# Attention steps reordered: scores, values, transposes, then a layer's products

## The chip, the cores and the metric

One core of a Trainium2 chip runs the whole program. The metric is the device time of one execution in microseconds, taken as the median of several runs. A profiled execution of the same program gives the trace; its time is the span from the first to the last instruction of the program.

## What is computed

A two-layer model on 256 latent and 256 context tokens of width 1024: layer 0 mixes tokens by retention, layer 1 by neighbourhood attention; each has a squared-ReLU MLP of hidden width 4096. The change lies in layer 1's attention, cut here to what matters:

```python
NAT_HEADS, NAT_HEAD_DIM, GRID_W, NAT_WIN_COLS = 32, 32, 64, 16
def row_block(args):                          # one row of 64 queries
    q_r, r = args
    k_band, v_band = ...                      # the rows of the window
    bias = jnp.where(col_in[:, None, :], bias, -jnp.inf)
    s_loc = jnp.einsum('bqhd,bikhd->bhqik', q_r, k_band) + bias
    s_ctx = jnp.einsum('bqhd,blhd->bhql', q_r, k_c)
    prob = jax.nn.softmax(jnp.concatenate([s_loc, s_ctx], -1), axis=-1)
    return (jnp.einsum('bhqik,bikhd->bqhd', p_loc, v_band)
            + jnp.einsum('bhql,blhd->bqhd', prob[..., band:], v_c))
y_lat = o.reshape(b, n, d) @ w_o
```

With 256 latent tokens there are four grid rows, all in every window. The columns of a window are 16 of 64.

## The kernel before

**Products in three parts.** Weights and activations are split into a high part (`hi`, rounded for the fast product) and a low part (`lo`, the rest); a product is three matmuls (`mm3`). `fetch(n)` (L255) issues the loads of the next `n` weight units from SP's queue (512 KB each) and casts each to `hi` on ScalarE (ACT); `lows(n)` (L277) subtracts on VectorE (DVE) to give `lo`. TensorE (PE) runs the products.

**An attention step** handles four heads (a group `g`) and one half of the query columns (`qt`), 16 steps in all. Each step `n` goes through these pieces:

- `scores(n)` (L1543): 12 matmuls in four 32-row tiles of the array, which write four PSUM banks (`pqk`), one a head.
- `soften(n)` (L1556): for each head VectorE adds the bias and takes the row minimum in one instruction (`s<-pqk,bias`), and ScalarE takes the exponential (`s<-s,mn`) with its row sum. `invert(n)` (L1582) takes the reciprocal of the sums and spreads them (`rr`).
- `gather(n)` (L1596): GpSimd copies the few probabilities of the other half's columns to one tile and loads a later step's bias.
- `flip(n)` (L1608): 13 transposes of the probabilities to four banks (`ppt`), three a head and a fourth one in the last; ScalarE copies the first and the third bank to `pt`, VectorE the second and the fourth. `flip_sums` (L1623) transposes the reciprocals to one half of the bank `pav`; `turned(n)` (L1629) copies them to `rt` on ScalarE.
- `attend(n)` (L1634), the values: one full-array matmul on the gathered probabilities and 12 matmuls in four 32-column tiles, accumulated in the other 128 columns of the same half of `pav`; then VectorE multiplies by `rt`, ScalarE casts the result to `oTh`, VectorE subtracts to `oTl`.

**Where TensorE's other work stands.** The loop at L1825 runs over 13 rows of `STEPS`. A turn runs `scores(n + 2)`, the values of step `n`, the transposes of step `n + 1`, and in `run(before)` a product of the layer: a K or Q or V part or a part of the output projection W, mostly 24 matmuls of 512 columns. `k_evac` and the like bring its result out of PSUM: a ScalarE cast (`kT<-pn`), then a VectorE subtraction. `K(6)`, `Q(3)` in turn 9 and `K(7)` in turn 11 make keys and queries for scores of turns 10 and 12. The first three numbers of a row of `STEPS` are the weight units fetched `early`, `late` and `last` in the turn.

**What sets the order.** Here the engines run what the code writes down, in that order; waits are semaphores put in by the framework. PSUM tiles come from one pool of eight banks (L144), of which `pav` is held through the whole stage; a bank is given out again when its readers are done.

```python
    STEPS = [                      # early, late, last, before, after
        (1, 0, 0, [K(2)], []),
        (0, 2, 0, [K(3)], []),
        (0, 2, 0, [K(4)], []),
        (0, 1, 0, [K(5)], []),
        (0, 2, 1, [Q(2)], []),
        (0, 1, 0, [V(0)], []),
        (0, 0, 0, [V(1)], []),
        (0, 0, 0, [V(2)], [REST]),
        (0, 0, 0, [V(3)], []),
        (2, 2, 1, [Q(3), K(6)], []),
        (0, 0, 1, [W00[0]], [W00[1]]),
        (0, 0, 2, [K(7)], []),
        (0, 0, 0, [W01[0]], [W01[1]]),
    ]
```

## Time and profile before

| | |
|---|---|
| median of 3 runs | 1182.22 us (1179.45 to 1182.62) |
| span of the profiled execution | 1177.4 us |
| TensorE busy | 1167.3 us, 99% of the span |
| VectorE, ScalarE, GpSimd busy | 844.6, 480.6, 212.5 us |
| memory read, rate over the span | 189.12 MB, 166 GB/s |

TensorE's clock is granted in full in all 40 slices of the page. In a timeline row stand start in us, length in us, engine, line, operation, tile written and tiles read, shapes and a count; several instructions in a row are merged to one, whose length then goes from the first's start to the last's end. A bracket gives idle time ahead and what ended it. All instructions carry L84, a helper that issues them; tile names tell them apart. A full-precision matmul shows as two passes (x2, x24). Ends of matmuls are modelled, so TensorE's waits are read from starts.

### The profile page before, as it was taken

What the parts mean: (1) busy time and instruction counts of PE and PEld (TensorE: products, weight loads), DVE (VectorE), ACT (ScalarE), POOL (GpSimd) and SP (SyncE); (2) the same over time, 40 slices, a digit from 0 to 9 for tenths busy, and PEclk for the clock granted to TensorE, in tenths of its full rate; (3) what the DMA queues carried; (4) which work ended last, traced back from release to release, by engine and by line L of the source; (5) the groups of instructions that cost most, each with busy time, mean ns of one, the idle gap of its engine ahead of it and who ended that gap; (6) DMA issues with size and microseconds to landing.
All of it is one profiled execution on the core that took longest, in us unless ns stands there. A gap on an engine that the chain in (4) does not pass through costs nothing.

```text
span 1177.4 us, 17745 instructions
## 1 busy us (share of the span) xinstructions
PE 1167.3 (99%) x6821; PEld 985.6 (84%) x6821; DVE 844.6 (72%) x1349; ACT 480.6 (41%) x819; POOL 212.5 (18%) x364
## 2 busy tenths in 40 slices
PE   9999999999999999999999999999999999999997
PEld 7788888888888889888888888889888878999886
DVE  3786678787888787757767675678577589877446
ACT  3643332222323246442212333137466666665341
POOL 0103001000200241780203000223343430000001
PEclk9999999999999999999999999999999999999999
DMA  9943544544355416757566665646344334766660
GB/s 276 276 130 104 161 143 140 152 147 152 118 169 175 141 60 214 189 112 217 171 190 197 212 199 190 201 141 204 83 135 139 111 115 155 222 209 197 233 212 36
DMA packets 140115, 195.10 MB, mean 166 GB/s; under 512 B 9936, under 2 KB 81136, under 8 KB 140032
## 3 DMA queue, kind: packets, MB, share of 16 engines
q1 hardware_dynamic: 131904, 182.03, 49.4%
q0 software_dynamic: 6976, 9.39, 3.9%
q10 hardware_dynamic: 1152, 2.56, 0.7%
q8 instruction: 53, 0.87, 0.3%
q14 instruction: 30, 0.25, 0.1%
HBM read 189.12 MB, written 5.75 MB: 166 GB/s over the span
## 4 chain that ended last, share of the span: by engine, by line
PE 94%; DMA 2%; SPq 1%; ACT 1%; DVE 1%; issue 0%; POOL 0%; ACTq 0%; DVEq 0%
PE p L84 44%; PE pw L84 7%; PE pg L84 7%; PE pq L84 7%; PE pv L84 7%; PE pn L84 5%; PE pnv L84 4%; PE po L84 3%; PE ppt L84 2%; PE pnw L84 1%; PE pS L84 1%; PE pav L84 1%; PE pqk L84 1%; SPq L84 1%; PE pt L84 1%; PE p1t L84 1%
## 5 line engine op out<-in xcount | busy, mean ns | idle before, releaser
L84 ACT CAST hi<-raw 128x1024 fp32r<-128x1024 f32 (+2 forms) x228 | 231.7, 1032 | 308.9 <-PE p L84 113.4
L84 DVE TENSOR_TENSOR lo<-raw,hi 128x1024 fp32r<-128x1024 f32 (+2 forms) x228 | 273.4, 1213 | 105.5 <-ACT hi L84 105.4
L84 PE MATMUL p<-hi,hid 128*128 128x512 f32 (+1 forms) x832 | 241.8, 373 | 0.0
L84 PEld LDWEIGHTS p<-hi,hid 128*128 128x128 f32 x832 | 152.1, 188 | 27.6
L84 PE MATMUL p<-hTh,lo 128*128 128x256 f32 (+1 forms) x512 | 165.8, 326 | 0.0
L84 PE MATMUL p<-hTl,hi 128*128 128x256 f32 (+1 forms) x512 | 165.8, 326 | 0.0
L84 PE MATMUL p<-hTh,hi 128*128 128x256 f32 (+1 forms) x512 | 162.9, 328 | 0.0
L84 PE MATMUL p<-lo,hid 128*128 128x512 f32 (+1 forms) x416 | 155.2, 373 | 0.0
L84 DVE SCALAR_TENSOR_TENSOR acc<-rawa,scol,acc 128x1024 f32<-128x1024 f32 x56 | 74.5, 1342 | 66.0 <-DMA rawa<-in_ada_w_dram 66.0
L84 PEld LDWEIGHTS p<-hTh,lo 128*128 128x128 f32 x512 | 96.4, 188 | 8.8
L84 PEld LDWEIGHTS p<-hTl,hi 128*128 128x128 f32 x512 | 96.4, 188 | 8.7
L84 PEld LDWEIGHTS p<-hTh,hi 128*128 128x128 f32 x512 | 94.2, 188 | 8.7
L84 PEld LDWEIGHTS p<-lo,hid 128*128 128x128 f32 x416 | 78.4, 188 | 13.7
L84 DVE SCALAR_TENSOR_TENSOR strips<-rawa,scol,strips 128x512 f32<-128x512 f32 x112 | 78.6, 762 | 0.0
L84 ACT CAST hid<-r 128x256 fp32r<-128x256 f32 (+1 forms) x64 | 31.9, 500 | 111.2 <-DVE r L84 111.2
L84 POOL TENSOR_TENSOR rstd<-rstd,misc 128x1 f32<-128x1 f32 x28 | 19.1, 684 | 212.4 <-DVE rstd L84 211.4
L84 POOL TENSOR_TENSOR R<-R,acc 128x512 f32<-128x512 f32 x16 | 25.8, 1633 | 168.8 <-DVE acc L84 168.8
L84 ACT ACTIVATE s<-s,mn 128x512 f32<-128x512 f32 x64 | 45.5, 713 | 22.0 <-DVE mn L84 22.0
L84 PE MATMUL pw<-hi,oh 128*128 128x512 f32 x128 | 51.0, 398 | 0.0
L84 PE MATMUL pg<-hi,hTh 128*128 128x512 f32 x128 | 50.6, 395 | 0.0
L84 PE MATMUL pq<-hTh,hi 128*128 128x512 f32 x128 | 49.3, 395 | 0.8 <-ACT hTh L84 0.5
L84 PE MATMUL pw<-hi,ol 128*128 128x512 f32 x128 | 49.9, 390 | 0.0
(238 smaller groups left out, 2278.5 us busy)
## 6 DMA issues: line engine op xcount, KB each, us to landing
raw<-in_mlp_w_dram SPq DMA_DIRECT2D x128, 512.0 KB, 4.2
rawa<-in_ada_w_dram SPq DMA_DIRECT2D x80, 512.0 KB, 3.9
raw<-in_ret_w_in_dram SPq DMA_DIRECT2D x42, 512.0 KB, 3.9
raw<-in_nat_w_in_dram SPq DMA_DIRECT2D x24, 512.0 KB, 4.3
rawq<-in_ada_w_dram SPq DMA_DIRECT2D x16, 512.0 KB, 6.2
raw<-in_ret_w_o_dram SPq DMA_DIRECT2D x16, 512.0 KB, 3.4
bias<-rpb_rows POOLq DMA_DIRECT2D x32, 128.0 KB, 2.9
raw<-in_nat_w_o_dram SPq DMA_DIRECT2D x8, 512.0 KB, 3.8
```

The lines of the kernel that those rows point to most:

```text
L84: r = f(*args, **kwargs)
```

## The change

In a turn the values and the transposes move ahead of the layer's product, directly behind the scores, values first. `soften` stands behind the transposes, `lows(early)` behind `soften`, `invert` behind the layer's product. Within `attend` the full-array matmul goes from the first place to the last.

```diff
@@ attend(n)
-        pe.matmul(po[:, :P], lhsT=rest_values(n), rhs=pt_at(n, NEAR), start=True, stop=False)
         for i, kc in enumerate((qt, 2, 3)):
             for j in range(4):
                 pe.matmul(
...
-                    start=False,
-                    stop=(i == 2),
+                    start=(i == 0),
+                    stop=False,
                     tile_position=(0, 32 * j),
                 )
+        pe.matmul(po[:, :P], lhsT=rest_values(n), rhs=pt_at(n, NEAR), start=False, stop=True)
@@ the loop over STEPS
         gather(n + 1)
         turned(n)
+        scores(n + 2)
+        attend(n)
+        flip(n + 1)
         fetch(early)
+        soften(n + 2)
         lows(early)
-        scores(n + 2)
-        soften(n + 2)
         fetch(late)
         lows(late)
         run(before)
-        flip(n + 1)
         invert(n + 2)
         fetch(last)
-        attend(n)
         run(after)
```

TensorE before, turn 3: from the third group of transposes to the scores of the next turn. The names are those of the pieces above; a wait names the semaphore of an engine (`Activation` is ScalarE).

```order
L84 MATMUL ppt_7631<-cst_81,s_7461 128x128 [waits DVE_49]
L84 MATMUL ppt_7631<-cst_81,s_7461 128x128 x2
L84 MATMUL ppt_7636<-cst_81,s_7464 128x128 [waits DVE_49]
L84 MATMUL ppt_7636<-cst_81,s_7464 128x128 x2
L84 MATMUL ppt_7636<-cst_81,pt_6946 128x128 [waits Pool_49]
L84 MATMUL pav_6943<-cst_81,rr_7529 128x128 [waits Activation_49]
L84 MATMUL pav_6943<-pt_6947,pt_6946 128x128
L84 MATMUL pav_6943<-pt_6947,natv_1079_6942 32x128 x12
L84 MATMUL pqk_7676<-kT_7234,qT_6598 128x512 [waits DVE_49]
```

TensorE in the changed kernel, the same turn, from the last of the scores to the fourth group of transposes:

```order
L84 MATMUL pqk_7561<-kT_7272,qT_6598 128x512
L84 MATMUL pav_6943<-pt_6947,natv_1079_6942 32x128 [waits Activation_49]
L84 MATMUL pav_6943<-pt_6947,natv_1079_6942 32x128 x11
L84 MATMUL pav_6943<-pt_6947,pt_6946 128x128
L84 MATMUL ppt_7590<-cst_81,s_7493 128x128 [waits DVE_49]
L84 MATMUL ppt_7590<-cst_81,s_7493 128x128 x2
L84 MATMUL ppt_7595<-cst_81,s_7496 128x128 [waits DVE_49]
L84 MATMUL ppt_7595<-cst_81,s_7496 128x128 x2
L84 MATMUL ppt_7600<-cst_81,s_7499 128x128 [waits DVE_49]
L84 MATMUL ppt_7600<-cst_81,s_7499 128x128 x2
L84 MATMUL ppt_7605<-cst_81,s_7502 128x128 [waits Activation_49]
```

The values stand ahead of the transposes, their first product waits for ScalarE and so does the fourth group of transposes, which waited for VectorE.

ScalarE in the changed kernel, from the last exponential of turn 4 on (`qT` brings out that turn's layer product, `rt` is `turned(5)`, `oTh` is the cast of `attend(5)`):

```order
L84 ACTIVATE s_7741,sums_7731<-s_7741,mn_7730 128x512 [waits DVE_49]
L84 CAST hi_7746<-raw_7744 128x1024 [waits DMAHW0_49]
L84 CAST hi_7751<-raw_7749 128x1024 [waits DMAHW1_49]
L84 ACTIVATE qT_6598<-pn_7756 128x256 [waits PE_49]
L84 ACTIVATE qT_6598<-pn_7757 128x256 [waits PE_49]
L84 CAST hi_7815<-raw_7813 128x1024 [waits DMAHW2_49,Activation_49]
L84 COPY rt_7827<-pav_6943 128x128 [waits Activation_49]
L84 CAST oTh_6944<-rt_7827 128x4x32 [waits DVE_49]
L84 COPY pt_6946<-ppt_7861 128x384 [waits PE_49,Activation_49]
```

Before, the copies to `pt` stood between `qT` and the last `hi`, and `oTh` ahead of `rt`; now the cast of the values stands between `rt` and the first copy to `pt`.

VectorE in turn 0, before:

```order
L84 COPY rr_7155<-sums_7039 128x128 [waits DVE_49]
L84 TENSOR_TENSOR lo_7201<-raw_7198,hi_7200 128x1024 [waits DMAHW2_49,PE_49,Activation_49]
L84 ISA s_7222,mn_7220<-pqk_7204,bias_6859 128x512 [waits DMASW1_49,DMASW6_49,DMASW0_49,DMASW7_49,PE_49,Pool_49]
L84 ISA mn_7220 128x1
L84 ISA s_7225,mn_7220<-pqk_7205,bias_6859 128x512 [waits PE_49,Pool_49]
```

And in the changed kernel:

```order
L84 COPY rr_7155<-sums_7039 128x128 [waits DVE_49]
L84 TENSOR_TENSOR rt_7196<-pav_6943,rt_7196 128x128 [waits PE_49,Activation_49]
L84 TENSOR_TENSOR oTl_6945<-rt_7196,oTh_6944 128x4x32 [waits Activation_49]
L84 COPY pt_6947<-ppt_7235 128x384 [waits PE_49]
L84 COPY pt_6947<-ppt_7245 128x512 [waits PE_49]
L84 ISA s_7259,mn_7257<-pqk_7198,bias_6859 128x512 [waits DMASW6_49,DMASW1_49,DMASW7_49,DMASW0_49,Pool_49]
L84 ISA mn_7257 128x1
```

The softening, which followed one subtraction, now follows the multiply of the values and the copies of the transposes, and the subtraction `lo` comes behind its fourth head.

## The prediction

> **What bounds the kernel now.** I read the page first, then the stretch of the attention steps (thirteen turns of the loop, 844 to 968 us) step by step, then the timeline of one engine at a time. TensorE runs without a gap and the chain of work that ended last lies on it:

> ```profile
> span 1177.4 us, 17745 instructions
> ...
> PE 94%; DMA 2%; SPq 1%; ACT 1%; DVE 1%; issue 0%; POOL 0%; ACTq 0%; DVEq 0%
> ```

> So whatever makes TensorE wait in these steps is paid in full. Busy time by step (columns: stretch, length, PE, PEld, DVE, ACT, POOL, granted clock, DMA share, GB/s) shows VectorE and ScalarE with two to four us free in each step:

> ```profile
> 853.08:862.20 9.12, 9.12 (x82) 7.38 (x78) 6.48 (x16) 6.64 (x15) 5.16 (x12) 1.00 0.37 84
> 880.59:890.48 9.89, 9.88 (x105) 8.85 (x102) 7.29 (x18) 6.80 (x17) 4.24 (x11) 1.00 0.48 128
> 890.48:900.23 9.75, 9.75 (x80) 7.73 (x77) 7.17 (x18) 6.24 (x15) 3.73 (x10) 1.00 0.65 192
> ```

> That free time is not a queue's slack: both engines work in order, and what counts is when one instruction is reached. One whole turn on TensorE, from the end of a layer's product to the start of the next:

> ```profile
> 868.44 0.39 PE L84 MATMUL pn<-hTh,lo 128*128 128x512 f32 x1
> 868.67 1.47 PE L84 MATMUL ppt<-cst,s 128*128 128x128 f32 x12
> 869.98 0.27 PE L84 MATMUL ppt<-cst,pt 128*128 128x128 f32 x1
> 870.09 0.27 PE L84 MATMUL pav<-cst,rr 128*128 128x128 f32 x1
> 870.20 0.39 PE L84 MATMUL pav<-pt,G 128*128 128x128 f32 x2
> 870.52 0.86 PE L84 MATMUL pav<-pt,natv 128*32 128x128 f32 x24
> 871.31 1.12 PE L84 MATMUL pqk<-kT,qT 32*128 32x512 f32 x12
> 872.36 0.50 PE L84 MATMUL pn<-hTh,hi 128*128 128x512 f32 x1
> ```

> Start to start: 0.23 us for a layer's product, 0.109 for a transpose, 14 transposes 1.53.

> **1. Array switches, about nothing.** A group's last start is its start + its length - the length of one product. Scores (32-row tiles) to the full array: 871.31 + 1.12 - 0.39 = 872.04, next at 872.36: 0.32. Full to 32-column tiles: 870.20 + 0.39 - 0.27 = 870.32, next at 870.52: 0.20. Columns to rows: 870.52 + 0.86 - 0.27 = 871.11, next at 871.31: 0.20. Two switches of the new order stand elsewhere:

> ```profile
> 843.65 0.39 PE L84 MATMUL pnv<-hi,hTl 128*128 128x512 f32 x1
> 843.97 0.97 PE L84 MATMUL pqk<-kT,qT 32*128 32x512 f32 x12
> ```

> ```profile
> 972.35 0.86 PE L84 MATMUL pav<-pt,R 128*32 128x128 f32 x24
> 973.14 1.09 PE L84 MATMUL ppt<-cst,s 128*128 128x128 f32 x8
> ```

> Full to rows 0.32; scores unhindered 0.97 - 0.39 = 0.58; columns to full 973.14 - (972.35 + 0.86 - 0.27) = 0.20. There are three switches a turn before and after. Rows to columns is not shown: between 0.20 and 0.38 (the wait less or more than the rows-to-full one by what the shown kinds differ); I take 0.32, since the same products have to leave. The quiet old turn of 9.12 less 1.53 (transposes), 0.32 (full product and switch), 0.59 + 0.20 (values and switch) and 0.58 + 0.32 (scores and switch) leaves 5.58 for the layer; 0.10 of it is the longer first product (872.36, 0.50 against 0.39) that follows a switch and 0.23 the step to the transposes, so from its first to its last start it takes 5.25 behind transposes. The new turn on TensorE alone, from the last layer product: 0.32 + 0.58 + 0.32 + 0.59 + 0.20 + 0.27 (the full product's two passes, with 0.05 for being first after a switch: 973.14 spaces its eight by 0.117) + 1.53 + 5.25 = 9.06. Thirteen times -0.06: **-0.8**. The tail gets one switch more (values now end full, then scores): +0.2.

> **2. What the old order waits for goes.** Scores followed values directly and waited for the copies of the transposes:

> ```profile
> 880.59 1.47 PE L84 MATMUL pqk<-kT,qT 32*128 32x512 f32 x12
> ```

> ```profile
> 890.48 1.61 PE L84 MATMUL pqk<-kT,qT 32*128 32x512 f32 x12
> 892.02 0.50 PE L84 MATMUL pnv<-hi,hTh 128*128 128x512 f32 x1
> ```

> Against 0.97: 0.15 + 0.50 + 0.64 = **-1.3**. Now a layer's product (5.2 us) stands before the scores.

> **3. The fourth group of transposes waits for a bank, each turn.** Eight banks, one held by `pav`; the four of the new scores stay full until VectorE softens them, which now stands behind the copies of the transposes. Three are left for four groups, and the order shows the fourth group waiting for ScalarE: the copy of the first. Before that copy ScalarE must cast the values:

> ```profile
> 879.10 0.58 ACT L84 CAST kT<-pn 128x512 fp32r<-128x512 f32 x1
> 879.57 0.85 ACT L84 COPY pt<-ppt 128x384 f32<-128x384 f32 x2
> 882.76 0.30 ACT L84 CAST oTh<-rt 128x128 fp32r<-128x128 f32 x1 [2.34 <-DVE rt L84]
> 882.97 0.26 ACT L84 COPY rt<-pav 128x128 f32<-128x128 f32 x1
> ```

> ```profile
> 872.15 1.14 DVE L84 COPY pt<-ppt 128x384 f32<-128x384 f32 x2
> 873.21 0.17 DVE L84 RECIPROCAL sums<-sums 128x4 f32<-128x4 f32 x1
> 873.48 0.23 DVE L84 COPY rr<-sums 128x128 f32<-128x128 f32 x1
> 873.63 0.28 DVE L84 TENSOR_TENSOR rt<-pav,rt 128x128 f32<-128x128 f32 x1
> ```

> From the start of the full product's second pass: 0.27 till it ends, 0.03 handover, 0.28 multiply, 0.03, 0.21 (cast, next start), 0.48 copy, 0.03 = 1.33. TensorE is there after 0.11 + 9 x 0.109 = 1.09. Wait 0.24, thirteen times: **+3.2**.

> **4. Values wait for `turned`, where ScalarE is late.** The order shows the first value product waiting for ScalarE: the copy `rt<-pav` out of the same bank, which stands behind the layer's evacuation and every cast fetched for later. Counted from the last layer product: 0.39 + 0.03 + 0.48 + 0.26 + 0.03 = 1.19; TensorE arrives after 0.32 + 0.58 + 0.32 = 1.22. A margin of 0.03: all lateness of ScalarE is paid. When is it late?

> ```profile
> 874.58 0.69 DVE L84 CUSTOM_DVE_ANT_1 s<-pqk,bias 128x512 f32<-128x512 f32 x1
> 875.20 0.08 DVE L84 DVE_READ_ACCUMULATOR2_ANT mn<- 128x1 f32 x1
> ```

> ```profile
> 886.28 0.71 ACT L84 ACTIVATE s<-s,mn 128x512 f32<-128x512 f32 x1
> 886.89 0.18 ACT L84 ACTIVATION_READ_ACCUMULATOR s<-s,mn 128x1 f32 x1
> 886.98 2.00 ACT L84 CAST hi<-raw 128x1024 fp32r<-128x1024 f32 x2
> ```

> Let A be the first value product; the full product's second pass starts 0.95 later (0.59 + 0.20 + 0.16), the fourth group 1.33 after that. It ends at A + 0.95 + 1.33 + 0.33 + 0.27 = A + 2.9; its copy on VectorE (0.60) and the first soften (0.69) with handovers give the first exponential at A + 4.25; four (0.71 each) end at A + 7.1; each late cast adds 0.95. The layer starts five products behind the fourth group's start, A + 2.85, and its last product is out at A + 2.85 + 5.25 + 0.39 = A + 8.5. With one late cast (A + 8.1) nothing is lost, with two (A + 9.0) 0.5. By `STEPS`: turns 1 and 2 (two late): 0.5 each, paid by the values of turns 2 and 3. Turn 4 (two late, one last): 0.5 + 0.95 = 1.5. Turn 7 has `REST` behind it, whose copies ScalarE takes in turns with VectorE:

> ```profile
> 920.53 0.26 ACT L84 COPY G<-pnv 32x128 f32<-32x128 f32 x1 [0.42 <-DVE pt L84]
> 921.22 0.26 ACT L84 COPY G<-pnv 32x128 f32<-32x128 f32 x1 [0.42 <-DVE pt L84]
> 921.50 0.27 ACT L84 COPY rt<-pav 128x128 f32<-128x128 f32 x1
> ```

> From its last product: 0.30 till ScalarE has it, three spacings of 0.69, 0.28 to the `rt` copy, 0.30 for that: 2.9; TensorE arrives after 0.20 + 0.58 + 0.32 = 1.1: 1.8, paid in turn 8. Turn 10 has half a layer (12 products), which ends at A + 5.8, while the exponentials and one cast need A + 8.1 and `rt` 0.3: TensorE arrives at A + 6.6, wait 1.8. Turn 11 casts two between evacuation and `rt`: 1.9, of which item 6 covers 1.1: 0.8. Sum 0.5 + 0.5 + 1.5 + 1.8 + 1.8 + 0.8 = **+6.9**. In four of these turns (2, 3, 5, 11) VectorE is late as well: its low parts, 1.14 each, begin at the first late cast's end, 0.95 before the second's; keys (0.60) and sums (0.42) follow, so its multiply starts 2.35 behind the second cast, and A stands 0.7 behind that cast: A + 1.65 in place of A + 1.25. The bank wait of item 3 grows by 0.4 there: **+1.6**.

> [...]

> **5. Low parts wait behind the softening.** `lows(early)` moved behind `soften`. VectorE:

> ```profile
> 879.22 1.23 DVE L84 TENSOR_TENSOR lo<-raw,hi 128x1024 fp32r<-128x1024 f32 x1 [2.11 <-ACT hi L84]
> 880.36 0.68 DVE L84 TENSOR_TENSOR kT<-pn,kT 128x512 fp32r<-128x512 f32 x1
> ```

> Softening starts at A + 3.5; four at 0.61, then 1.23: A + 7.2. In turn 0 the fifteenth product of the layer needs it at A + 2.85 + 14 x 0.227 = A + 6.0: 1.2. In turn 9, whose first layer has half-wide products (26 x 0.116): 1.3. **+2.5**.

> **6. Keys just in time.** Turn 10 opens with scores on `K(6)`, turn 12 on `K(7)`, each the product right before; transposes and values stood between (868.67 to 871.31, 2.6 us). Now: 0.39 + 0.03 + 0.58 + 0.03 = 1.03 against the switch's 0.32, then the low part on VectorE 0.68 + 0.03 against four scores' 0.3: 0.7 + 0.4 = 1.1, twice: **+2.2**.

> Cost at nothing: the moved `fetch` and its DMA issues (SP issues far ahead of use; if that cover went, a landing of 4 us would show as a wait of a cast), POOL's `gather` (same place in the turn; its copies must end before the fourth group's last transpose, 2.6 us after the scores start).

> Sum: -0.8 + 0.2 - 1.3 + 3.2 + 6.9 + 1.6 + 2.5 + 2.2 = **+14.5**. The profiled execution takes 1177.4 us of span; the median of the runs is 1182.2, 4.8 above it, which the change does not touch. Forecast: 1182.2 + 14.5 = **1196.7**.

> **The rivals.** (a) *Not slower: the waits for ScalarE are for work long done.* The order names the engine that a product waits for, not the instruction. If values and the fourth transposes wait only for copies of the turn before, which are 8 us old when TensorE arrives, items 3 and 4 are nothing: +2.8, 1185.0, which a measurement can't tell from before; with a cheap switch (its bound, 13 x 0.12 less) 1183.4. It decides by when ScalarE is through with `rt` and the first group's copy: from 1.22 us behind the layer's last product and 1.09 behind the full product down, nothing waits. Against it stand the order in ScalarE's queue and the count of banks, three for four groups. Chance 0.06. (b) *ScalarE in time*: item 4's 8.5 vanish, the rest stays: +6.0, 1188.2. For it speaks that ScalarE is idle 2.5 to 3.5 us a turn; against it, that this idle time lies ahead of the exponentials. Chance 0.12. (c) *The handovers cost more*: 0.08 in place of 0.03. The five of item 3 and of the way on to TensorE add 0.25 a turn, and item 4's margin of 0.03 goes in the eight quiet turns (three handovers, 0.12 each): +4.2, 1200.9. Chance 0.12. (d) The forecast, 0.70: 1192 to 1200, with rows to columns at its bounds (1.6 lower, 0.8 higher) and the larger waits 2 us either way.

> **The numbers.** About 0.3% (3.5 us) is what a measurement can tell from no change. (b), (c) and (d) are slower by more than that, 0.94 together; (a) is within it but for 0.01 on its lower side. The range, 1187 to 1203, reaches from (b) past (c) and leaves out (a) and some tails.

> **What would show it.** In the profile after, turns of 9.3 us where quiet, 10 to 12 in turns 0, 2, 3, 5, 8 and 11; a gap of 0.24 ahead of the tenth transpose; `pav` waiting for ScalarE's `rt`; scores of turns 10 and 12 waiting for `kT`. Turns near 9.06 without these gaps would prove it wrong.

## The result, and the profile after

The changed kernel takes 1197.66 us (median; 1197.31 to 1202.21), the kernel before in the same comparison 1180.84 us: the ratio is 1.0159, 95% interval 1.0144 to 1.0173, slower. (That ratio is the recorded estimate; the quotient of the two medians is 1.0142.) The forecast was 1196.7. That it came within 1 us is luck: two errors of the forecast offset each other in that number, as the account below shows.

The page's first line and the line of shares of the chain that ended last, of the changed kernel:

```profile
span 1200.1 us, 17737 instructions
...
PE 90%; DVE 4%; ACT 3%; issue 2%; DMA 1%; POOL 1%; DVEq 0%; ACTq 0%; SPq 0%
```

TensorE is still the chain, but with 90% in place of 94%; VectorE and ScalarE now stand on it with 7% together, where they had 2%. In the stage the engines do the same work and take longer for it. The whole of the thirteen turns before, then after (columns: stretch, length, busy time of PE, PEld, DVE, ACT, POOL with counts, granted clock, DMA share, GB/s):

```profile
843.97:968.20 124.23, 124.09 (x1092) 101.77 (x1091) 86.86 (x222) 80.76 (x197) 51.02 (x126) 1.00 0.43 124
```

```profile
847.07:990.74 143.67, 129.98 (x1092) 102.57 (x1091) 87.77 (x222) 82.12 (x197) 53.37 (x126) 0.98 0.38 107
```

1092 matmuls in both, and 19.44 us more. TensorE's idle time grows from 0.14 to 13.7 us, and the granted clock, which was full, is 0.98. By turn, from the start of one step's scores to the next (us):

| turn | 0 | 1 | 2 | 3 | 4 | 5 | 6 | 7 | 8 | 9 | 10 | 11 | 12 |
|---|---|---|---|---|---|---|---|---|---|---|---|---|---|
| before | 9.11 | 9.12 | 9.11 | 9.28 | 9.89 | 9.75 | 9.14 | 9.55 | 9.12 | 15.14 | 6.42 | 9.11 | 9.49 |
| after | 10.86 | 9.51 | 10.30 | 10.25 | 9.80 | 11.19 | 9.54 | 10.08 | 12.60 | 17.40 | 7.27 | 12.42 | 12.45 |

TensorE's waits in the stage after (in all, how often, the longest); before, it was idle for 0.14 us in the whole stage:

```profile
PE pav L84 <- ACT rt L84: 6.0, 6, 1.8
PE ppt L84 <- ACT pt L84: 3.4, 11, 0.7
PE pn L84 <- DVE lo L84: 2.2, 2, 1.1
PE pqk L84 <- ACT kT L84: 1.4, 2, 0.7
PE pqk L84 <- DVE kT L84: 0.4, 2, 0.2
```

Six value groups wait for ScalarE's `rt` (the forecast's item 4), eleven fourth groups of transposes for ScalarE's copy (item 3), two products for a low part (item 5), and two groups of scores for the keys (item 6). These idle times count from modelled ends; counted from starts, as below, the same waits are somewhat longer. A quiet turn (turn 1) on TensorE, from the last layer product to the next layer's first:

```profile
857.61 0.39 PE L84 MATMUL pn<-hTh,lo 128*128 128x512 f32 x1
857.93 0.98 PE L84 MATMUL pqk<-kT,qT 32*128 32x512 f32 x12
858.85 0.86 PE L84 MATMUL pav<-pt,natv 128*32 128x128 f32 x24
859.64 0.49 PE L84 MATMUL pav<-pt,pt 128*128 128x128 f32 x2
859.96 1.15 PE L84 MATMUL ppt<-cst,s 128*128 128x128 f32 x9
861.29 0.55 PE L84 MATMUL ppt<-cst,s 128*128 128x128 f32 x3 [0.18 <-ACT pt L84]
861.67 0.27 PE L84 MATMUL ppt<-cst,pt 128*128 128x128 f32 x1
861.78 0.27 PE L84 MATMUL pav<-cst,rr 128*128 128x128 f32 x1
```

Ends of matmuls are modelled, so the starts tell the wait: nine transposes at 0.109 from 859.96 end with a next start at 860.94, and the tenth starts at 861.29: 0.34 lost, here and in every other quiet turn. (Turns 8 and 12 have no such wait: their twelve transposes run at half clock, those of turn 12 in part, and take 2.77 and 2.10 us; this comes up below.) The other two engines in that time:

```profile
860.23 0.29 DVE L84 TENSOR_TENSOR rt<-pav,rt 128x128 f32<-128x128 f32 x1 [0.47 <-PE pav L84]
```

```profile
860.56 0.30 ACT L84 CAST oTh<-rt 128x128 fp32r<-128x128 f32 x1 [1.77 <-DVE rt L84]
860.76 0.92 ACT L84 COPY pt<-ppt 128x384 f32<-128x384 f32 x2
```

ScalarE stands idle for 1.77 us, because the cast of the values comes ahead of the copy and waits for VectorE's multiply. The first group of transposes is in its bank before that wait ends: in a kernel below that copies at once, the copy starts 0.58 us behind the group's first transpose, which here would be 860.54, and it starts at 860.76. The first copy is through at about 861.24 (0.48 from 860.76), and 0.05 later the fourth group starts.

### The profile page after: what moved, and what is told of

Its sections match the earlier page's. It is cut to its first block, busy times and chain, and to the rows that moved or that the text cites. A ratio compares the mean times of both kernels' runs of the same rounds, so it can differ in the third digit from the quotient of the medians.

```text
span 1200.1 us, 17737 instructions
## 1 busy us (share of the span) xinstructions
PE 1176.4 (98%) x6821; PEld 988.9 (82%) x6821; DVE 847.6 (71%) x1349; ACT 481.1 (40%) x819; POOL 214.9 (18%) x364
## 4 chain that ended last, share of the span: by engine, by line
PE 90%; DVE 4%; ACT 3%; issue 2%; DMA 1%; POOL 1%; DVEq 0%; ACTq 0%; SPq 0%
PE p L84 43%; PE pq L84 8%; PE pv L84 7%; PE pg L84 6%; PE pw L84 6%; PE pnv L84 4%; PE pn L84 3%; PE po L84 2%; PE pnw L84 2%; PE pav L84 1%; PE pS L84 1%; PE ppt L84 1%; PE pada L84 1%; PE pt L84 1%; ACT s L84 1%
## 5 line engine op out<-in xcount | busy, mean ns | idle before, releaser
L84 ACT CAST hi<-raw 128x1024 fp32r<-128x1024 f32 (+2 forms) x228 | 231.7, 1032 | 302.5 <-PE p L84 119.5
L84 DVE TENSOR_TENSOR lo<-raw,hi 128x1024 fp32r<-128x1024 f32 (+2 forms) x228 | 274.9, 1219 | 98.6 <-ACT hi L84 98.4
L84 PE MATMUL p<-hi,hid 128*128 128x512 f32 (+1 forms) x832 | 241.8, 373 | 0.0
L84 PEld LDWEIGHTS p<-hi,hid 128*128 128x128 f32 x832 | 152.2, 188 | 27.8
L84 PE MATMUL p<-hTh,lo 128*128 128x256 f32 (+1 forms) x512 | 165.8, 326 | 0.0
L84 PE MATMUL p<-hTl,hi 128*128 128x256 f32 (+1 forms) x512 | 165.8, 326 | 0.0
L84 PE MATMUL p<-hTh,hi 128*128 128x256 f32 (+1 forms) x512 | 162.9, 328 | 0.0
L84 PE MATMUL p<-lo,hid 128*128 128x512 f32 (+1 forms) x416 | 155.2, 373 | 0.0
L84 DVE SCALAR_TENSOR_TENSOR acc<-rawa,scol,acc 128x1024 f32<-128x1024 f32 x56 | 74.9, 1349 | 61.8 <-DMA rawa<-in_ada_w_dram 61.6
L84 PEld LDWEIGHTS p<-hTh,lo 128*128 128x128 f32 x512 | 96.4, 188 | 8.8
L84 PEld LDWEIGHTS p<-hTl,hi 128*128 128x128 f32 x512 | 96.4, 188 | 8.6
L84 PEld LDWEIGHTS p<-hTh,hi 128*128 128x128 f32 x512 | 94.2, 188 | 8.8
L84 PEld LDWEIGHTS p<-lo,hid 128*128 128x128 f32 x416 | 78.4, 188 | 13.5
L84 DVE SCALAR_TENSOR_TENSOR strips<-rawa,scol,strips 128x512 f32<-128x512 f32 x112 | 78.5, 762 | 0.0
L84 ACT CAST hid<-r 128x256 fp32r<-128x256 f32 (+1 forms) x64 | 31.9, 500 | 108.7 <-DVE r L84 108.7
L84 POOL TENSOR_TENSOR rstd<-rstd,misc 128x1 f32<-128x1 f32 x28 | 19.1, 685 | 212.0 <-DVE rstd L84 211.0
L84 POOL TENSOR_TENSOR R<-R,acc 128x512 f32<-128x512 f32 x16 | 25.8, 1629 | 168.9 <-DVE acc L84 168.9
L84 ACT ACTIVATE s<-s,mn 128x512 f32<-128x512 f32 x64 | 45.5, 712 | 20.7 <-DVE mn L84 20.7
L84 PE MATMUL pw<-hi,oh 128*128 128x512 f32 x128 | 51.0, 398 | 0.0
L84 PE MATMUL pg<-hi,hTh 128*128 128x512 f32 x128 | 50.6, 395 | 0.0
L84 PE MATMUL pw<-hi,ol 128*128 128x512 f32 x128 | 50.1, 391 | 0.5 <-DVE ol L84 0.5
L84 PE MATMUL pg<-hi,hTl 128*128 128x512 f32 x128 | 49.9, 390 | 0.0
```

The source lines that it names most:

```text
L84: r = f(*args, **kwargs)
```

## The experiments

Each kernel is the changed kernel with the edit shown, unless another base is named. The ratio is to the kernel before, timed in the same comparison (its median was 1179.2 to 1180.8 in all of them); the stage is that of the profiled execution, and the last column counts its stretches of half clock inside the stage, which come up below.

| kernel | us | ratio (95%) | stage, us | half clock |
|---|---|---|---|---|
| before | 1180.84 | 1 | 124.23 | 0 |
| changed | 1197.66 | 1.0159 (1.0144 to 1.0173) | 143.67 | 2 |
| product last, old order | 1180.86 | 1.0008 (0.9996 to 1.0020) | 125.52 | 0 |
| new order, product first | 1199.53 | 1.0162 (1.0141 to 1.0183) | 142.63 | 1 |
| `rt` copied early | 1196.37 | 1.0144 (1.0123 to 1.0166) | 140.74 | 1 |
| split of values late | 1195.46 | 1.0132 (1.0112 to 1.0153) | 139.33 | 1 |
| late casts first | 1196.04 | 1.0141 (1.0126 to 1.0156) | 138.77 | 0 |
| early low parts first | 1194.89 | 1.0123 (1.0108 to 1.0138) | 139.97 | 1 |
| `rt` early, split late | 1190.65 | 1.0103 (1.0086 to 1.0120) | 135.66 | 0 |
| softening first | 1200.08 | 1.0177 (1.0159 to 1.0195) | 145.10 | 2 |
| the same, keys later | 1200.99 | 1.0186 (1.0171 to 1.0201) | 148.47 | 3 |
| softening in halves | 1196.04 | 1.0127 (1.0111 to 1.0143) | 141.13 | 2 |
| halves, `rt`, split, keys | 1188.80 | 1.0080 (1.0064 to 1.0096) | 132.38 | 0 |
| halves, `rt`, split, early units | 1187.54 | 1.0060 (1.0046 to 1.0074) | 133.76 | 1 |

(With keys later, scores move within turns 10 and 12, so its two stages begin and end at the same pieces but no single turn compares.) Kernels whose intervals overlap are not told apart by their time. Of the four edits tried alone below (`rt` early, split late, late casts first, early low parts first) only the last is clear of the changed kernel; for the other three the evidence is in the turns of the trace.

### The two parts of the change, each alone

The loop of the kernel before, with only this in `attend`:

```diff
-        pe.matmul(po[:, :P], lhsT=rest_values(n), rhs=pt_at(n, NEAR), start=True, stop=False)
...
+        pe.matmul(po[:, :P], lhsT=rest_values(n), rhs=pt_at(n, NEAR), start=False, stop=True)
```

> The loop order of the kernel before, with only the full product of a values group moved from its start to its end. Theory (order of the pieces makes the loss, the product's place next to nothing): full to columns, columns to full, full to rows in place of full to columns, columns to rows, so one switch more a turn, 0.20 us and 0.05 for the product that follows it, 13 x 0.25 = 3.3 us: about 1184.1 us where the kernel before takes 1180.8, and no new wait in the trace. Rival (a values group that ends on the full array is what costs): 1190 us or more.

Then the new loop with that edit undone.

> The changed kernel's loop order, with the full product of a values group back at its start. Theory: the waits for rt, for the fourth bank, for lo and for kT all stay; one switch more a turn (0.20) of which the fourth group's wait for a bank takes back about 0.1: 1197 to 1200 us, the stage of thirteen turns 143 to 146 us long. Rival (the product's place is what costs): within 4 us of the kernel before, 1181 to 1185 us.

The product's place is worth next to nothing in either order: 1.0008 against 1, and 1.0162 against 1.0159. So the order of the pieces makes the loss. (The stage of the second, 142.63 us, is a little under the expected 143 to 146, with one stretch of half clock where the changed kernel has two.) In the old order the extra switch is there all the same. Turn 2 of product-last-alone, and its turn 4:

```profile
862.18:871.49 9.31, 9.31 (x78) 7.41 (x77) 6.33 (x16) 6.51 (x15) 3.17 (x8) 1.00 0.56 165
880.79:890.38 9.59, 9.59 (x101) 8.70 (x100) 6.99 (x18) 7.07 (x17) 3.67 (x10) 1.00 0.45 125
```

9.31 against 9.11 is 0.2 us a turn, 2.6 in thirteen; but turn 4 falls from 9.89 to 9.59, since scores come later and no longer wait for copies. Turns 3, 4, 5 and 12, in which TensorE had waits before, take 0.55 us less together and not 0.8 more: the old waits swallow half the price, and 125.52 - 124.23 = 1.29 us is left. The expectation of 3.3 had priced the switch and forgotten the waits that it covers.

### The wait for `rt`, removed

```diff
-        turned(n)
+        if n == 0:
+            turned(0)
         scores(n + 2)
         attend(n)
         flip(n + 1)
+        turned(n + 1)
```

> The changed kernel with the copy rt<-pav of step n+1 issued right behind the transposes of step n+1, a turn earlier, ahead of the exponentials and late casts on ScalarE. Theory: the first value product waits for that copy because of its place in ScalarE's queue: 6.4 us of waits ahead of value products go, and the two stretches of half clock that follow the two longest waits with them (up to 3 us in the executions that have them): 1188 to 1191 us; the fourth group's wait for a bank stays, 0.3 to 0.8. Rival (the first value product waits for something else that is late, the bank itself or values): 1196 to 1199 us. Rival (the half clock comes whatever the waits): stretches of half clock stay, 1191 to 1193 us.

The expectation failed: 1196.37 us. Turns 2, 3 and 5, in which those waits had stood:

```profile
863.02:873.29 10.27, 9.50 (x77) 7.23 (x76) 7.36 (x18) 6.58 (x16) 4.94 (x12) 1.00 0.54 155
873.29:883.59 10.30, 9.52 (x79) 7.24 (x78) 7.39 (x18) 6.38 (x15) 3.67 (x10) 1.00 0.55 158
893.32:904.49 11.17, 9.31 (x79) 7.25 (x78) 8.27 (x20) 7.07 (x17) 3.35 (x9) 1.00 0.65 191
```

They were 10.30, 10.25 and 11.19: 31.74 us together in either kernel. The waits are all still there; they stand elsewhere. Turn 5 of this kernel on TensorE, VectorE and ScalarE:

```profile
895.33 1.15 PE L84 MATMUL ppt<-cst,s 128*128 128x128 f32 x9
898.34 0.55 PE L84 MATMUL ppt<-cst,s 128*128 128x128 f32 x3 [1.86 <-ACT pt L84]
```

```profile
892.80 2.36 DVE L84 TENSOR_TENSOR lo<-raw,hi 128x1024 fp32r<-128x1024 f32 x2 [2.10 <-ACT hi L84]
...
896.15 1.22 DVE L84 TENSOR_TENSOR lo<-raw,hi 128x1024 fp32r<-128x1024 f32 x1
897.29 0.28 DVE L84 TENSOR_TENSOR rt<-pav,rt 128x128 f32<-128x128 f32 x1
```

```profile
897.61 0.30 ACT L84 CAST oTh<-rt 128x128 fp32r<-128x128 f32 x1 [2.41 <-DVE rt L84]
```

The values start on time now, but VectorE comes to their multiply only at 897.29, behind three low parts that waited for the late casts; ScalarE's `oTh` waits 2.41 us for it, the first copy stands behind `oTh`, and the fourth group behind the copy. So in these turns two engines are late side by side, ScalarE at `rt` and VectorE at the multiply, both because of the same late casts, and taking one away shows the other. Where ScalarE alone was late, the edit pays: turns 8 and 12 take 10.35 and 10.57 us here, against 11.35 and 11.31 in the next kernel, which has these waits. Turn 11, where VectorE is late too, takes 13.99 where the changed kernel took 12.42: its wait moved to the fourth group as well (2.16 us), and a stretch of half clock falls into it.

### The late casts, moved

If the casts are the common root, moving them into ScalarE's idle time ahead of the exponentials should free both engines:

```diff
         fetch(early)
+        fetch(late)
         soften(n + 2)
         lows(early)
-        fetch(late)
         lows(late)
```

> The changed kernel with fetch(late) ahead of the softening, so that ScalarE casts late units in its idle time before the exponentials. New theory, after the copy of rt was moved early and the waits turned up in the same turns, and as long, at the fourth group of transposes: ScalarE as a whole is late there (exponentials, then casts, then the evacuation), and whichever of its copies TensorE needs next waits. Turns 1, 2 and 4 cast two late units: turns 2, 3 and 5 fall from 10.30, 10.25 and 11.19 us to about 9.5, 9.5 and 10.2, the rest stays: 2.5 us less than the changed kernel, about 1195. Rival (the casts wait for their DMA, wherever they are issued): no change, or the exponentials wait for the DMA and all turns 2, 3, 5 get longer, 1198 us or more.

Turns 2, 3 and 5 of this kernel:

```profile
864.02:873.52 9.50, 9.32 (x77) 7.25 (x76) 7.47 (x17) 6.60 (x15) 5.94 (x13) 1.00 0.57 157
873.52:883.03 9.51, 9.33 (x78) 7.25 (x77) 6.39 (x16) 5.76 (x14) 4.70 (x12) 1.00 0.65 176
892.83:903.07 10.24, 9.39 (x78) 7.25 (x77) 7.68 (x19) 6.49 (x15) 4.41 (x10) 1.00 0.84 211
```

The three numbers are the expected ones: turns 2 and 3 are quiet turns now, and what turn 5 keeps is the last unit's cast between `qT` and `rt`. The theory had put the lateness on ScalarE alone; by the rows above the engine behind the moved wait is VectorE, but both hang on the casts. The median is 1 us over the expected one, and its interval overlaps that of the changed kernel.

### The split behind the copies, and both together

```diff
-        attend(n)
+        attend(n, False)         # without the cast oTh and the subtraction oTl
         flip(n + 1)
+        halves(n)                # these two
```

> The changed kernel with the cast oTh<-rt and the subtraction oTl of a values group issued behind the copies of the transposes instead of ahead of them. Theory: ScalarE, which waited for VectorE's multiply before it could copy the first group of transposes, copies at once and the fourth group finds its bank: the gap ahead of the tenth transpose falls from 0.34 (0.6 to 0.8 in turns 2, 3, 5, 11) to 0.1 or less, 4.5 to 5.5 us in all: 1192 to 1193 us; the waits for rt stay. Rival (the fourth group waits for the scores' banks or for VectorE's copies): no change, 1196 to 1199 us.

Turn 1 of this kernel:

```profile
856.38 0.49 PE L84 MATMUL pav<-pt,pt 128*128 128x128 f32 x2
856.71 1.66 PE L84 MATMUL ppt<-cst,s 128*128 128x128 f32 x12
858.20 0.27 PE L84 MATMUL ppt<-cst,pt 128*128 128x128 f32 x1
```

From the first to the thirteenth transpose 858.20 - 856.71 = 1.49 us, where it was 861.67 - 859.96 = 1.71 and twelve at 0.109 are 1.31; the quiet turn falls from 9.51 to 9.31. A little over half of the wait is gone: the first copy now starts as soon as its group is written, and that is still 0.13 too late. So the place of `oTh` in ScalarE's queue, which the forecast named, makes 0.2 of the 0.34; the rest stays with three banks for four groups, even if the copy starts at once. The gain in the median, 2.2 us, is less than the 4.5 expected, and the trace shows where some went: in turn 5 values now wait 1.40 us for `rt` instead of 1.20 (0.8 more over turns 2, 3, 5 and 11), because everything ahead of them got shorter and ScalarE did not; and the products of turns 0 and 9 wait 0.4 more for low parts.

With `rt` early as well:

> The changed kernel with both edits that were tried alone: rt copied early, and the cast oTh behind the copies of the transposes. Recorded theory (two waits for two separate copies, whose costs add up): 8.5 + 4.8 less, 1184 to 1186 us. New theory (ScalarE is late as a whole, and its first copy of the transposes now meets the late casts and evacuations itself): in turns 2, 3, 5, 8 and 11 the fourth group still waits 0.4 to 1.8, 5 us in all; quiet turns are 9.2 to 9.3: 1190 to 1193 us.

1190.65 us, within the range of the new theory. Its account by turn holds in part: the fourth group waits only 0.2 to 0.4 us (turns 2, 3, 5, 11), and the longer waits stand elsewhere, 0.93 and 1.18 us at the transposes of the reciprocals in turns 5 and 11 and 0.77 in turn 8 ahead of the full product. Alone the two edits take 0.0015 and 0.0027 off the ratio, together 0.0056, some 7 us, far from the 13.3 of the recorded sum. The longest wait that is left in turn 5 names the same multiply:

```profile
896.61 0.33 PE L84 MATMUL pav<-cst,rr 128*128 128x128 f32 x1 [0.76 <-DVE rt L84]
```

The transpose of the reciprocals writes one half of `pav` and the multiply reads the other, and the transpose waits for it, 0.76 us by this row: different columns of one bank, and a wait all the same. The wait is one of the framework's semaphores, so the row shows the order that the program keeps; what the two would do at once is not shown.

### The low parts of turns 0 and 9

```diff
         fetch(early)
-        soften(n + 2)
         lows(early)
+        soften(n + 2)
```

> The changed kernel with lows(early) ahead of the softening; only turns 0 and 9 have early units. Theory: the waits of a product for lo, 1.22 us in turn 0 and 1.30 in turn 9, go, turn 0 falls from 10.86 to 9.7 or less and turn 9 from 17.40 to 16.2; the softening of those turns comes 1.2 and 2.5 us later, for which nothing waits in turn 0: 1195 to 1196 us, the trace's stage 2.4 us shorter. Rival (the later softening makes ScalarE later and the wait turns up behind the layer, as with rt): turns 0 and 1, or 9 and 10, together as long as before, no change.

Turns 0 and 9 after the change, then in this kernel:

```profile
847.07:857.93 10.86, 9.61 (x77) 7.16 (x76) 5.33 (x13) 5.70 (x14) 3.27 (x8) 1.00 0.16 40
941.20:958.60 17.40, 15.41 (x125) 13.06 (x124) 9.50 (x19) 9.78 (x21) 7.83 (x14) 1.00 0.55 147
```

```profile
843.23:852.75 9.52, 9.34 (x79) 7.26 (x78) 5.34 (x13) 5.71 (x14) 1.23 (x4) 1.00 0.18 55
936.02:952.24 16.22, 15.37 (x126) 12.95 (x126) 9.58 (x19) 9.78 (x21) 5.51 (x13) 1.00 0.50 148
```

1.34 and 1.18 us less, turns 1 and 10 as in the changed kernel (9.50, 7.29): item 5 is shown, at 2.5 us, and nothing takes its place.

### The softening's place

Would the softening directly behind the scores, where the kernel before had it, take all waits away at once?

```diff
         scores(n + 2)
+        soften(n + 2)
         attend(n)
         flip(n + 1)
         fetch(early)
-        soften(n + 2)
```

> The changed kernel's order on TensorE (scores, values, transposes, layer; product last) with one difference: soften(n+2) is issued directly behind scores(n+2), as in the kernel before, and not behind the transposes. New theory: the loss comes from the softening's place behind values and transposes on VectorE, which starts the exponentials 3 to 4 us later and so makes ScalarE late at the end of the layer; with it back, the waits for rt, for the fourth bank and for lo vanish together, the waits for kT (1.1 twice) stay: turns of 9.1 to 9.2 us, the stage about 126 us, 1181 to 1184 us. Rival (TensorE's own order costs, or VectorE's copies of the transposes, now behind four softenings, make TensorE wait for banks): 1190 us or more.

No: 1200.08 us, the rival. Turn 2 of this kernel on TensorE and on VectorE:

```profile
867.77 0.27 PE L84 MATMUL ppt<-cst,pt 128*128 128x128 f32 x1
869.42 0.33 PE L84 MATMUL pav<-cst,rr 128*128 128x128 f32 x1 [1.38 <-DVE rt L84]
```

```profile
868.47 0.69 DVE L84 CUSTOM_DVE_ANT_1 s<-pqk,bias 128x512 f32<-128x512 f32 x1
869.08 0.08 DVE L84 DVE_READ_ACCUMULATOR2_ANT mn<- 128x1 f32 x1
869.08 0.29 DVE L84 TENSOR_TENSOR rt<-pav,rt 128x128 f32<-128x128 f32 x1
```

The multiply of the values now stands behind four softenings, and the transpose into `pav` waits for it. In the kernel before, transposes and values stood a layer's product (5.3 us) behind the scores, and the softening was done by then; with values right behind the scores, VectorE has two urgent things at one time, and either order of them makes TensorE wait. How long depends on when VectorE gets there: in turns 0, 6 and 7 it softens as soon as the scores are written, and this wait is 0.44 us from start to start; in turns 1 to 5, where it comes about 1 us later, it is 1.2 to 1.5. With the scores of turns 10 and 12 set behind the transposes besides:

> The same, and in turns 10 and 12 alone, whose scores need the keys made right before, values and transposes stand ahead of scores and softening. Theory: the waits of scores for kT (0.74 + 0.39, twice) go, one array switch more in each (0.2 to 0.3): 1.5 us less than with the softening's place alone, 1179.5 to 1182 us. Rival (the keys are late by more than 2.6 us, or rt is the next wait): no difference from it.

1200.99, no gain: its rival. The waits for `kT` go, those of the transposes at `pav` stay, and `rt` is the next wait: the values that now stand first in turns 10 and 12 wait 1.94 and 2.89 us for it.

Two heads softened ahead of the multiply and two behind it:

```diff
         scores(n + 2)
+        soften(n + 2, (0, 1))
         attend(n)
+        soften(n + 2, (2, 3))
         flip(n + 1)
         fetch(early)
-        soften(n + 2)
```

> The changed kernel's order on TensorE; the softening of heads 0 and 1 is issued directly behind the scores and that of heads 2 and 3 directly behind the values' multiply, ahead of the copies of the transposes. Softening all four heads first had moved the wait to the transpose of the reciprocals into pav, which waited until VectorE, behind four softenings, had multiplied the values. Theory: two softenings (1.3 us) fit into the time in which TensorE runs values, so the multiply isn't late; two of the scores' banks come free before the fourth group of transposes wants one; exponentials start 3 us earlier, so that ScalarE is through with casts before the layer ends, and VectorE takes lo in time: quiet turns 9.2 us, turns 2 and 3 the same, lo waits of turns 0 and 9 gone, while the waits behind the cast of turn 4's last unit, behind turn 7's copies and for kT stay: 1184 to 1187 us. Rival (VectorE has no slack for the multiply, whatever the split): the transpose into pav waits 0.4 or more in each turn, 1190 us or more.

Its turns 1 and 6 reach 9.19 and 9.14 us, the expected 9.2, but turns 2 and 3 take 10.63 and 10.14: behind two late low parts VectorE comes late to the softening, and the fourth group waits for that. In turn 2 another 0.48 us comes on top, in which VectorE waits for the load of a bias:

```profile
867.06 0.69 DVE L84 CUSTOM_DVE_ANT_1 s<-pqk,bias 128x512 f32<-128x512 f32 x1 [0.48 <-DMA G<-rpb_rows]
```

In turns 0 and 9, products wait for `hi`, since the early cast now stands behind exponentials. 1196.04 us, a miss of ten. The time is in the rival's range, but the rival itself (a wait in each turn) is not what the quiet turns show. Then all edits that had helped, with the split softening:

> The same, with rt copied a turn earlier, the cast oTh behind the copies of the transposes, and in turns 10 and 12 values and transposes ahead of scores. Theory: now that ScalarE is not late as a whole, the wait for rt in turns 5, 8 and 12 doesn't turn up elsewhere, and the waits for kT go: 4 to 6 us less than with the split softening alone, 1179 to 1182 us, about the kernel before. Rival (the waits move once more, as they did with rt alone): less than 2 us gained.

1188.8 us, seven over the range that was expected. It gains 7 us on the kernel before it, more than expected, but from a start that was ten too high. The last kernel, with early units at the start of the turn and scores first throughout:

> The split softening, rt copied a turn earlier and the cast oTh behind the copies of the transposes, as in the last combination; scores stay first in turns 10 and 12 too, and fetch(early) with lows(early) stand at the start of the turn, as in the kernel before. Theory: the waits for the early units' cast and lo (0.56 + 0.69 in turn 0, 0.37 + 0.92 in turn 9) go, 2.5 us; the waits that came with scores set later in turns 10 and 12 (2.00, 0.68, 0.68) give way to those for kT (1.1 twice), 1 us: 1184.5 to 1186 us, still 5 us over the kernel before: 2.2 of it for kT, 0.7 for the copies of turn 7, 2 for VectorE's low parts in turns 2, 3 and 5. Rival (each edit moves a wait and none goes): 1188 us or more.

1187.54 us, the lowest of the new order, between the expectation and its rival, and not told apart from the one before it (the intervals overlap). Turn 0 shows why the early units gave little:

```profile
845.46 1.22 DVE L84 TENSOR_TENSOR lo<-raw,hi 128x1024 fp32r<-128x1024 f32 x1 [3.48 <-ACT hi L84]
846.71 0.69 DVE L84 CUSTOM_DVE_ANT_1 s<-pqk,bias 128x512 f32<-128x512 f32 x1
```

VectorE waits 3.48 us for the cast of a unit, and the softening waits behind it; the fourth group then waits 0.83 us for the softening, in turn 9 1.69. No kernel in the new order came nearer than 0.6% to the old one. Late casts first was not tried together with `rt` early and the split late; whether that would come nearer is open.

## Why the forecast was right, and where it was not

Direction and size came from the right places; the sum of terms was too low and the base too high. The measured sizes, from the trace after:

| step of the forecast | forecast, us | measured, us | from |
|---|---|---|---|
| 1. switches, in the turns | -0.8 | +0.7 | quiet turn 9.51 - 0.34 = 9.17, was 9.12 |
| 2. old score waits | -1.3 | -1.3 | scores of turns 3, 4, 5 of before; none after |
| 3. bank for the fourth group | +3.2 | +4.4 | 13 x 0.34 (see below the table) |
| 4. values wait for `rt` | +6.9 | +6.4 | gaps 0.49, 0.46, 1.20, 1.86, 1.77, 0.66 |
| 4. bank wait grows | +1.6 | +1.5 | 0.63, 0.63, 0.83, 0.72 less 0.34 each |
| 5. low parts | +2.5 | +2.5 | gaps 1.22, 1.30 |
| 6. keys | +2.2 | +2.5 | (0.74 + 0.49) twice |
| half clock | none | +2.4 | turns 8 and 12, below |
| sum in the stage | +14.3 | +19.1 | of 19.44 |

Item 3's wait is seen in eleven turns. In turns 8 and 12 the slower transposes cover it, and the price of the half clock is taken there over turns that have it, so that the two rows together count once. The half clock is read from the one execution that was profiled: of the other three only the mean granted clock is known, 0.996 to 0.998 against 0.995, so they had less of it, in the stage or behind the end of TensorE's work, and they agree within 0.6 us. Without it the stage's loss is 17.0 us, and the medians differ by 16.8; that the others had none in the stage is not shown.

**Item 1** was mis-sized by 0.11 a turn, 1.5 us. The two passes of the full product take 0.32 (859.64 to 859.96) where 0.27 was allowed, and the three transposes that start behind the wait 0.38 (861.29 to 861.67) where 0.33 was. The switch from rows to columns, for which the forecast had to choose between 0.20 and 0.38, took 0.33 (858.52, the last start of the scores, to 858.85).

**Item 3** was mis-sized by 0.10 a turn (and 13 x 0.24 is 3.1, not 3.2). With item 1 this makes the quiet turn 9.51 us where the forecast has 9.3. The forecast counted 1.33 us from that second pass to the fourth group; it took 1.44: the second pass ends the two of 0.32 and starts at 859.85, and the group starts at 861.29. The handover to VectorE is the larger part: 0.38 from there to the multiply's start at 860.23, where 0.30 was counted. The late split shows the part of `oTh`, 0.2 of the 0.34; that the rest is the count of banks is argued from the semaphore on ScalarE's copy.

**Item 4** has the right turns (2, 3, 5, 8, 11, 12) and nearly the right sizes, and the causes by turn held: two late casts, the last unit's cast, `REST`, the half layer. What fell is that it is one wait with one cure. The forecast had VectorE's lateness as a small extra on the fourth group; it is a second path, just as late, and `rt` out of the way only uncovers it. The part that the late casts cause, in turns 2, 3 and 5, is shown by moving them; that of turn 8, the place of `rt` behind the copies of `REST`, by copying `rt` early (10.35 us against 11.35, with 0.77 of a new wait for one of those copies); that of turn 11 by the size alone.

**Item 5** is shown by undoing it. **Item 6** is seen in the trace: scores start 0.74 late, and their twelve starts spread over 1.07 us and not 0.58, since four wait for the low part. Setting the scores later in turns 10 and 12 took those waits away, but no run shows a gain from that alone.

**The rivals.** (a), waits for work long done, and (b), ScalarE in time, fall to 6.0 us of waits for `rt` in six turns. (c), slower handovers, was right for one of item 3's five (0.08 more); in the quiet turn above the first value product follows the scores after the switch alone, so the margin for `rt` held. What was forecast at nothing, the moved loads and GpSimd's copies, shows up in no wait of TensorE in the changed kernel.

**The base** was the step that went wrong without harm. The forecast took the difference between the profiled span (1177.4) and the median of three runs (1182.2), 4.8 us, for time around the span. In the changed kernel each run's time stands 2.0 to 2.1 over its own span (1202.21 and 1200.1), and the run of 1179.45 is 2.05 over 1177.4: the profiled execution was that one, and 2.8 us were the spread between runs. From 1179.4, the forecast's 14.5 would have given 1193.9, 3.6 us short of 1197.5, where three of the four runs lie (1197.31 to 1197.87): in the range still, but the agreement within 1 us is the two errors together.

The profiled execution of the changed kernel is the fourth, 4.7 us over those. Most of that lies outside the change: the stage starts 3.1 us later than before (847.07 against 843.97), with a program that is the same up to there (in all the other kernels here it starts at 842.7 to 843.9), and 2.9 of it are lost in the first 128 matmuls (20.00 us, before 17.10).

## What to carry to other kernels

When a wait is to be priced, look for every engine that would be late at that place, not for the one the profile names: the price is that of the latest, and it goes only when all of them are early, best by the work that made them late together. Work that feeds a later product can stand far from its consumers or close to them; put directly behind the scores, values and softening compete for VectorE at the same moment, and no order of the two found here was free. A median of three runs is a weak base for a forecast: over 7 to 17 runs the kernel before has medians of 1179.2 to 1179.7 us, close to the 1179.45 of the profiled run.

## What the hardware did that was not expected

```profile
929.05:932.46 3.41, 1.62 (x38) 0.98 (x31) 1.40 (x8) 1.04 (x4) 1.34 (x3) 1.00 0.30 66
932.46:935.87 3.41, 3.41 (x17) 3.34 (x16) 1.51 (x4) 1.26 (x3) 0.00 (x0) 0.50 0.00 0
976.83:980.25 3.42, 2.03 (x16) 0.81 (x14) 1.88 (x4) 2.60 (x4) 3.25 (x6) 1.00 0.42 105
980.25:983.66 3.41, 3.31 (x33) 2.87 (x34) 0.84 (x3) 0.69 (x3) 0.00 (x0) 0.50 0.52 171
```

Inside such a stretch a group of twelve transposes takes nearly twice its time (1.47 us in the kernel before):

```profile
932.48 2.77 PE L84 MATMUL ppt<-cst,s 128*128 128x128 f32 x12
```

The price is to be had by comparing turns with the same instructions and waits: turn 8 takes 12.60 us here and 11.35 where the late casts come first, turn 12 takes 12.45 and 11.31, and both of the latter are at full clock:

```profile
922.66:934.01 11.35, 9.39 (x81) 7.25 (x77) 6.01 (x22) 5.46 (x17) 4.11 (x11) 1.00 0.16 38
971.08:982.39 11.31, 10.02 (x103) 7.33 (x104) 8.01 (x21) 7.90 (x18) 2.74 (x8) 1.00 0.26 74
```

1.25 + 1.14 = 2.4 us. The two falls are 47.79 us apart, 14 times 3.41 within the rounding, as if the clock were decided on a fixed grid; that a wait costs the half clock or not by where it falls on it is the author's reading of this distance, and not shown. With the split late, a wait for `rt` in turn 8 of the same 1.85 us fell otherwise on the grid that goes back from that kernel's own fall at 961.54 (eleven stretches, to 924.00), and no half clock followed:

```profile
924.00:927.41 3.41, 1.63 (x33) 1.43 (x32) 1.32 (x7) 0.87 (x4) 1.02 (x2) 1.00 0.22 47
```

TensorE's busy time alone doesn't tell the two apart: a fall behind 2.03 us, none behind 1.63. The other two falls came behind 1.50 us (split late, 958.13 to 961.54) and 1.25 (`rt` early, 961.50 to 964.91); none came behind 1.70 us in the changed kernel (966.59 to 970.00) and 1.72 with `rt` early (896.65 to 900.06). What decides it stays open.
